# Side work of a hybrid decoder layer issued in the order of how it uses the matmul array: halves of columns, halves of rows, the whole array

## The chip, the core and the metric

The kernel runs on one core of one Trainium2 chip. The metric is the device time of one execution in microseconds (us). The engines that matter are PE (TensorE, the matmul array), DVE (VectorE), ACT (ScalarE), POOL (GpSimd) and SP (SyncE, which issues most of the DMAs). Each works through its own instructions in the program's order and meets the others only at semaphores.

## The reference

One pre-norm decoder layer on x of 512 positions by 1024 features, in float32:

```
u = rmsnorm(x);  proj = u @ w_in            # q, k, v, pool_in, z, xbc, dt, gates
y_a = dilated_attention(q, k, v) @ w_a      # 3 groups of 6 heads of 64, softmax with a bias
y_b = causal_pooling(pool_in) @ w_b
y_c = ssd(z, xbc, dt) @ w_c                 # Mamba-2 scan, 16 heads, 4 chunks of 128 positions
x = x + (g0 * y_a + g1 * y_b + g2 * y_c) @ w_o
x = x + conv_ffn(rmsnorm(x));  out = rmsnorm(x)
```

## The kernel before

The dense products are made of matmuls with 128x128 weights and 512 columns. Each float32 operand is split into a high and a low part, and a product is three runs of matmuls (high by high, high by low, low by high), all issued by `mm3` (L230). Their results are the tiles pa, pb, pqk, pu, ppw and p in four PSUM banks. A list of jobs, one for each block of weights, gives their order. Weights arrive by DMA (raw, L179), ACT rounds them (wh, L191), and DVE forms the low part (wl, L211), some jobs ahead. The program fixes by hand the order in which PE, ACT, DVE and POOL issue.

Attention, the SSD scan and the norms are side work, written as Python generators. After each chunk of the dense stream a job calls `step()`: it finishes the second halves of casts (`flush`), moves each running generator on to its next `yield`, oldest first, and then starts one new generator from `waiting`. So a generator's stages are spread over steps, and the steps' matmuls stand between the chunks of the stream.

Two kinds of generators meet the change most. An attention item (`item` in `attend`) is one head of a bank. The even head of a pair issues the scores of both heads (ps, L656), where each head uses 64 of the array's 128 rows. Each head then adds the bias and finds the maximum on DVE (L663, L664, L666, or L670, L674) and takes the exponential on ACT (L677). Two steps later the probabilities are transposed with the whole array (pt, L683), and DVE (even head) or ACT (odd head) copies them to SBUF (L684). One step after the odd head's transposes come the products with v (po, L695), where each head fills 64 of 128 columns, and ACT copies the result when it is complete (L701). An SSD item (`ssd_item`) fetches decay rows (al and ea, L913 and L919), transposes x (pxs, L923) and forms C by B (pcb, L929); DVE and ACT form a masked decay (L940, L941, L945); its last stage has products in halves of columns (py, L955), then whole products (pyo, L961; pst, L972), and DVE joins them (L963 to L977). Other whole-array side products are pcs, pact, pbt, pss, prb and the transposed statistics.

All side products share four further PSUM banks (tag "sm"): a product waits until the reader of an earlier tile has left its bank.

Of the kernel before, what the change touches and what calls it, by code (L numbers as in the profile page):

```python
# [83 lines left out]
def trunk(ctx: ExitStack, tc, out, x, rel_bias, ln1_g, w_in, b_gate, w_a, pool_w, pool_scale, w_b,  # L84
# [29 lines left out]
    def SM(name):  # L114
        return psum.tile([P, S], F32, name=name, tag="sm")
# [9 lines left out]
    waiting, running = [], []  # L125
# [13 lines left out]
    def flush():  # L139
        todo = second[:]  # L140
        second.clear()
        for f in todo:
            f()

    def step():
        flush()
        for it in list(running):
            try:
                next(it)
            except StopIteration:  # L150
                running.remove(it)
        if waiting:
            it = iter(waiting.pop(0))
            running.append(it)
            try:
                next(it)
            except StopIteration:
                running.remove(it)

    def after(n, it):  # L160
        for _ in range(n):
# [386 lines left out]
    def bias_of(g, h):  # L548
        if g == 0:
            return bias[h // 2][:, (h % 2) * 256:(h % 2) * 256 + 256]  # L550
        o = 256 * (g - 1) + (h % 2) * P
        return bias[3 + h // 2][:, o:o + P]
# [80 lines left out]
    def attend(g):  # L633
        nm = cpool.tile([P, 4, HEADS], F32, name=f"nm{g}")
        ls = cpool.tile([P, 4, HEADS], F32, name=f"ls{g}")
        if g == 0:
            banks = [[(1, 0, 2), (2, 1, 2)], [(3, 2, 2), (0, 0, 1)]]
        else:
            banks = [[(n, n, 1) for n in range(4)]]
        outs, probs, scores = {}, {}, {}  # L640

        def item(h, nb, bank):
            c, hh = h // 2, h % 2
            b = bias_of(g, h)
            off, spans = 0, []
            for n, kb, w in bank:
                spans.append((n, kb, w, off))
                off += w * P
            if hh == 0:

                q, k = QK["q", g, c], QK["k", g, c]
                pss = [SM("ps"), SM("ps")]
                for n, kb, w, o in spans:
                    for i in range(2):
                        r = slice(DH * i, DH * i + DH)
                        pe.matmul(pss[i][:, o:o + w * P], q[r, n * P:(n + 1) * P],  # L656
                                  k[r, kb * P:(kb + w) * P], start=True, stop=True)
                scores[c, nb] = pss
            ps = scores[c, nb][hh]
            total = off  # L660
            sb = T("sb")
            if g == 0 and total == 384:
                dve.tensor_tensor(sb[:, :256], ps[:, :256], b, OP.add)  # L663
                dve.tensor_tensor(sb[:, 256:384], ps[:, 256:384], b[:, P:], OP.add)  # L664
                for n, kb, w, off in spans:
                    dve.tensor_reduce(nm[:, n, h:h + 1], sb[:, off:off + w * P],  # L666
                                      AX.X, OP.max, negate=True)
            else:
                n = len(bank)
                dve.tensor_tensor(sb.rearrange("p (n c) -> p n c", n=n),  # L670
                                  ps.rearrange("p (n c) -> p n c", n=n),
                                  b.unsqueeze(1).to_broadcast([P, n, S // n]), OP.add)
                n0 = bank[0][0]
                dve.tensor_reduce(nm[:, n0:n0 + n, h], sb.rearrange("p (n c) -> p n c", n=n),  # L674
                                  AX.X, OP.max, negate=True)
            for n, kb, w, off in spans:
                act.activation(sb[:, off:off + w * P], sb[:, off:off + w * P], AF.Exp,  # L677
                               bias=nm[:, n, h:h + 1], accum_out=ls[:, n, h:h + 1])
            yield
            yield  # L680
            pt = SM("pt")
            for o in range(0, total, P):
                pe.transpose(pt[:, o:o + P], sb[:, o:o + P], eye)  # L683
            (act.copy if h % 2 else dve.tensor_copy)(sb[:, :total], pt[:, :total])  # L684
            probs[h, nb] = sb
            if h % 2 == 0:
                return
            yield
            if c not in outs:
                outs[c] = SM("po")  # L690
            po = outs[c]
            for n, kb, w, off in spans:
                for i in range(w):
                    for hh in range(2):
                        pe.matmul(po[DH * hh:DH * hh + DH, n * P:(n + 1) * P],  # L695
                                  V[g, kb + i][:, (2 * c + hh) * DH:(2 * c + hh + 1) * DH],
                                  probs[2 * c + hh, nb][:, off + i * P:off + (i + 1) * P],
                                  start=i == 0, stop=i == w - 1)
            if nb == len(banks) - 1:
                o = T(f"o{g}")  # L700
                act.copy(blocked(o, g), grouped(po, g))  # L701
                OT[g, c] = o

        def stats():
            for src, store, nme in ((nm, NM, "nmT"), (ls, LS, "lsT")):
                ps = SM("pst")
                for n in range(4):
                    pe.transpose(ps[:HEADS, n * P:(n + 1) * P], src[:, n, :], eye)
                t = T(nme)
                dve.tensor_copy(blocked(t[:HEADS], g), grouped(ps[:HEADS], g))  # L710
                store[g] = t
            return
            yield

        fill([item(2 * c + hh, nb, bank) for c in range(3) for nb, bank in enumerate(banks)
              for hh in range(2)] + [after(2, stats())])

    AO = []
# [109 lines left out]
    def ssd_prep():  # L828
# [33 lines left out]
        dve.scalar_tensor_tensor(v4(a), v4(dtv), -1.0, bc(1), OP.mult, OP.mult)  # L862
        yield
        yield
        ps = SM("pcs")
        pe.matmul(ps[:, :n16], tri, a, start=True, stop=True)
        pe.matmul(ps[:, n16:2 * n16], ones, a, start=True, stop=True)
# [7 lines left out]
        act.activation(dec, dec, AF.Exp)  # L875
        act.activation(tot, tot, AF.Exp)
        yield
        pt = SM("pact")
        for c in range(4):
            pe.transpose(pt[:SH, c * P:(c + 1) * P], acs[:, c * SH:(c + 1) * SH], eye)  # L880
        at, et = T("acst"), T("east")
# [13 lines left out]
    btok, prev, done = {}, {}, set()  # L895

    def btok_item(gi):
        ps = SM("pbt")
        for c in range(4):
            pe.transpose(ps[:, c * P:(c + 1) * P], XS[8 + gi][:, c * P:(c + 1) * P], eye)  # L900
        t = btok[gi] = T("btok")
        act.copy(t, ps)
        return
        yield

    def ssd_item(c, gi):
        cs = slice(c * P, (c + 1) * P)
# [7 lines left out]
        if c:  # L915
            ea = T("ea")
            for i in range(2):
                h0 = 8 * gi + i
                sp.dma_start(ea[DH * i:DH * i + DH].rearrange("p (j l) -> p j l", j=4),  # L919
                             ed[h0:h0 + 8 - i:2, cs].partition_broadcast(DH))  # L920
        ps = SM("pxs")
        for j in range(4):
            pe.transpose(ps[:, j * P:(j + 1) * P], XS[4 * gi + j][:, cs], eye)  # L923
# [28 lines left out]
        for j in range(4):  # L952
            for i in range(2):
                o, lo = (2 * j + i) * DH, (2 * j + i) % 4 * P
                pe.matmul(py[DH * i:DH * i + DH, j * P:(j + 1) * P], xc[:, o:o + DH],  # L955
                          als[j // 2][:, lo:lo + P], start=True, stop=True)
        by_j = lambda t: t.rearrange("p (j l) -> p j l", j=4)
        if c:
            po = SM("pyo")
            for j in range(4):  # L960
                pe.matmul(po[:, j * P:(j + 1) * P], prev[gi][:, j * P:(j + 1) * P], XS[10 + gi][:, cs],  # L961
                          start=True, stop=True)
            dve.tensor_tensor(ea, po, ea, OP.mult)  # L963
            dve.tensor_tensor(ea, ea, py, OP.add)
# [49 lines left out]
    def y_norm(gi):  # L1014
        while len(SQ[gi]) < 4:
            yield
        yield
        yield
        ps = SM("pss")
        for tb in range(4):  # L1020
            pe.matmul(ps[:, tb:tb + 1], SQ[gi][0][:, tb * P:(tb + 1) * P], ones[:, :1],
                      start=True, stop=True)
        r = rstd_of(ps[:, :4], 4, S)
        dg = T("dg")
        dve.tensor_tensor(dg.rearrange("p (b t) -> p b t", b=4), eye.unsqueeze(1).to_broadcast([P, 4, P]),
                          r.unsqueeze(2).to_broadcast([P, 4, P]), OP.mult)
        yield
        yield
        yield
        ps = SM("prb")  # L1030
        pe.matmul(ps, ones, dg, start=True, stop=True)
        for j in range(4):
            y, m = Y[gi][:, j, :], 4 * gi + j
            dve.scalar_tensor_tensor(y, y, cst["dgc"][:, 8 + m:9 + m], ps, OP.mult, OP.mult)
            yh, yl = T("yth", F32R), T("ytl", F32R)
            act.copy(yh, y)
            YT[m] = (yh, yl)
            if j % 2:
                yield
                for q in (m - 1, m):  # L1040
                    dve.tensor_sub(YT[q][1], Y[gi][:, q % 4, :], YT[q][0].bitcast(F32))
# [614 lines left out]
```

## Time and profile before

| | |
|---|---|
| median of 3 runs | 1048.81 us (1046.5 to 1051.13) |
| the profiled execution, its own time | 1049.47 us |
| its span, first to last instruction | 1047.4 us |
| mean granted clock of PE | 0.997 |
| instructions | 13090, of which 5220 matmuls |

In the timeline of an engine each row gives the start in us from the start of the span, the duration in us, the engine, the source line, the operation, the output and inputs by the program's names, and the number of equal instructions merged into the row; a bracket gives idle time before it and what ended that. The form 64*128 or 128*64 of a matmul is rows by columns of the array in use. A matmul's duration includes its passage through the array, so starts are compared, not durations.

### The profile page before, as it was taken

Reading aid. Unit: us, or ns where it says so; the run is one execution under the profiler, and the core shown is the slowest. Engines: PE = TensorE matmul, PEld = TensorE weight load, DVE = VectorE, ACT = ScalarE, POOL = GpSimd, SP = SyncE. Lnnn points to the kernel's source line nnn. Section 1 sums busy time; section 2 is a strip of 40 time slices with the busy share of each in tenths; the row PEclk is TensorE's granted clock in tenths of the full one; section 3 lists DMA queues with packets and bytes.
Section 4 is the critical chain, followed back from the end, with each engine's and each line's share of the span. In section 5 each row is a group of like instructions: output and inputs, shape, how many; then the busy total and the mean of one; then the engine's idle time right before and its main releaser. Section 6 shows DMA issues by size and latency. Waiting matters only on the chain.

```text
span 1047.4 us, 13090 instructions
## 1 busy us (share of the span) xinstructions
PE 1036.3 (99%) x5220; PEld 864.5 (83%) x5220; DVE 642.6 (61%) x865; ACT 467.6 (45%) x753; POOL 138.0 (13%) x118
## 2 busy tenths in 40 slices
PE   8999999999999999999999999999999999999997
PEld 8988877898888887787888888898888888878885
DVE  4563565774356647676658856766766566556645
ACT  5432555452474363557554324545444343433331
POOL 1680000000000001100143500001111111110110
PEclk9999999999999999999999999999999999999999
DMA  8445222127222363542252426643232322362322
GB/s 254 145 111 152 97 65 74 31 59 202 81 81 81 82 159 101 152 130 59 65 151 81 161 81 223 222 156 107 81 121 81 116 86 89 112 241 66 115 101 81
DMA packets 119787, 121.80 MB, mean 116 GB/s; under 512 B 5523, under 2 KB 101590, under 8 KB 119727
## 3 DMA queue, kind: packets, MB, share of 16 engines
q1 hardware_dynamic: 119135, 120.12, 37.1%
q8 instruction: 41, 0.67, 0.3%
q10 hardware_dynamic: 592, 0.86, 0.3%
q14 instruction: 19, 0.16, 0.0%
HBM read 115.07 MB, written 4.32 MB: 114 GB/s over the span
## 4 chain that ended last, share of the span: by engine, by line
PE 92%; DVE 3%; DMA 2%; ACT 2%; issue 0%; DVEq 0%; SPq 0%; ACTq 0%
PE pa L230 35%; PE pu L230 22%; PE pb L230 13%; PE pqk L230 9%; PE pa L1508 2%; PE p L230 2%; DVE wl L211 2%; PE ps L656 1%; PE po L695 1%; PE pt L683 1%; DMA raw<-in_ffn_w_up_dram 1%; PE ppw L230 1%; ACT wh L191 1%; PE py L955 1%; DMA raw<-in_w_o_dram 1%; PE pyo L961 1%
## 5 line engine op out<-in xcount | busy, mean ns | idle before, releaser
L211 DVE TENSOR_TENSOR wl<-raw,wh 128x2048 fp32r<-128x2048 f32 (+3 forms) x95 | 218.5, 2301 | 77.7 <-ACT wh L191 40.3
L191 ACT CAST wh<-raw 128x1024 fp32r<-128x1024 f32 (+3 forms) x188 | 189.6, 1026 | 67.4 <-DVE raw L333 21.1
L230 PE MATMUL pa<-uh,wh 128*128 128x512 f32 x384 | 98.7, 399 | 0.0
L1165 DVE SCALAR_TENSOR_TENSOR hc<-pu,fcol,hc 128x510 f32<-128x510 f32 x88 | 65.9, 748 | 50.8 <-ACT hc L1162 49.2
L230 PE MATMUL pa<-uh,wl 128*128 128x512 f32 x384 | 95.0, 389 | 0.0
L230 PE MATMUL pa<-ul,wh 128*128 128x512 f32 x384 | 94.9, 389 | 0.0
L230 PEld LDWEIGHTS pa<-ul,wh 128*128 128x128 f32 x384 | 72.1, 188 | 15.2
L230 PEld LDWEIGHTS pa<-uh,wl 128*128 128x128 f32 x384 | 72.0, 188 | 15.2 <-DVE wl L211 0.3
L230 PE MATMUL pu<-uh,wh 128*128 128x512 f32 (+1 forms) x352 | 83.7, 380 | 0.2 <-ACT uh L448 0.2
L230 PE MATMUL pu<-ul,wh 128*128 128x512 f32 (+1 forms) x352 | 83.5, 379 | 0.0
L230 PE MATMUL pu<-uh,wl 128*128 128x512 f32 (+1 forms) x352 | 83.5, 379 | 0.0
L230 PEld LDWEIGHTS pa<-uh,wh 128*128 128x128 f32 x384 | 70.2, 188 | 15.3 <-issue 1.0
L230 PEld LDWEIGHTS pu<-uh,wh 128*128 128x128 f32 x352 | 64.1, 188 | 12.8 <-ACT uh L448 0.4
L230 PEld LDWEIGHTS pu<-ul,wh 128*128 128x128 f32 x352 | 64.2, 188 | 12.5
L230 PEld LDWEIGHTS pu<-uh,wl 128*128 128x128 f32 x352 | 64.2, 188 | 12.5
L1162 ACT ACTIVATE hc<-pu,fcol,fcol 128x512 f32<-128x512 f32 x40 | 31.2, 780 | 75.5 <-PE pu L230 75.3
L1170 POOL TENSOR_TENSOR hc<-hc 128x512 f32<-128x512 f32 x22 | 31.5, 1432 | 223.6 <-DVE hc L1165 169.4
L934 POOL TENSOR_TENSOR xd<-xc,dec 128x512 f32<-128x512 f32 x6 | 6.4, 1065 | 360.1 <-DVE xc L925 334.5
L677 ACT ACTIVATE sb<-sb,nm 128x128 f32<-128x128 f32 (+1 forms) x72 | 30.1, 419 | 24.1 <-DVE nm L674 17.2
L1050 ACT ACTIVATE sg<-pa,col 128x512 f32<-128x512 f32 x24 | 16.5, 687 | 50.7 <-PE pa L230 50.6
L230 PE MATMUL pqk<-uh,wh 128*128 128x512 f32 x144 | 36.9, 394 | 0.0
L230 PE MATMUL pqk<-ul,wh 128*128 128x512 f32 x144 | 36.3, 389 | 0.0
(348 smaller groups left out, 1751.7 us busy)
## 6 DMA issues: line engine op xcount, KB each, us to landing
raw<-in_w_in_dram SPq DMA_DIRECT2D x25, 1024.0 KB
raw<-in_ffn_w_up_dram SPq DMA_DIRECT2D x22, 1024.0 KB
raw<-in_w_in_dram SPq DMA_DIRECT2D x20, 512.0 KB
raw<-in_ffn_w_down_dram SPq DMA_DIRECT2D x10, 1024.0 KB
raw<-in_w_o_dram SPq DMA_DIRECT2D x8, 1024.0 KB
raw<-in_w_b_dram SPq DMA_DIRECT2D x4, 1024.0 KB
al<-ad SPq DMA_DIRECT2D x16, 256.0 KB
raw<-in_w_c_dram SPq DMA_DIRECT2D x4, 1024.0 KB
```

What stands on the lines that cost most here:

```text
L191: act.copy(job.high[:, :, o], job.raw[:, :, o])
L211: (eng or dve).tensor_tensor(l[:, :, o], job.raw[:, :, o], h[:, :, o].bitcast(F32), OP.subtract)
L230: pe.matmul(ps, l, r, start=first and n == 0, stop=last and n == total - 1)
L656: pe.matmul(pss[i][:, o:o + w * P], q[r, n * P:(n + 1) * P], k[r, kb * P:(kb + w) * P], start=True, stop=True)
L677: act.activation(sb[:, off:off + w * P], sb[:, off:off + w * P], AF.Exp, bias=nm[:, n, h:h + 1], accum_out=ls[:, n, h:h + 1])
L683: pe.transpose(pt[:, o:o + P], sb[:, o:o + P], eye)
L695: pe.matmul(po[DH * hh:DH * hh + DH, n * P:(n + 1) * P], V[g, kb + i][:, (2 * c + hh) * DH:(2 * c + hh + 1) * DH], probs[2 * c + hh, nb][: ...
L1050: act.activation(s, ps, AF.Sigmoid, bias=col[:, o:o + 1])
L1162: act.activation(t, ps, AF.Identity, bias=ff["c1"][:, ff["b"] + m:ff["b"] + m + 1], scale=fw(2, m))
L1165: dve.scalar_tensor_tensor(t[:, sh:], ps[:, :S - sh], fw(k, m), t[:, sh:], OP.mult, OP.add)
L1170: pool.tensor_tensor(a, a, t, OP.mult)
L1508: pe.matmul(first[2 * n + j][:, lo:hi], a[:, k, j * P:(j + 1) * P], b[:, k, lo:hi], start=a is wh and b is uh and k == 0, stop=a is wl and ...
```

## The change

A generator may now yield a phase, `ROWS` or `WHOLE`, ahead of matmuls of that kind. `step()` takes the new generator in first, and then goes over all of them three times: in phase 0 each goes on until a bare `yield` (the end of its step) or until it names a later phase; those that named `ROWS` go on next, those that named `WHOLE` last. So all products in halves of columns of a step come first, then the scores, then everything that uses the whole array. Whatever a generator does for ACT, DVE, POOL or SP between these points moves with it. In particular, the odd head's bias, maximum and exponentials have no matmul before them, so they are issued in phase 0, ahead of the transposes and copies of older generators in the same step.

```diff
     def step():
         flush()
-        for it in list(running):
-            try:
-                next(it)
-            except StopIteration:
-                running.remove(it)
         if waiting:
-            it = iter(waiting.pop(0))
-            running.append(it)
-            try:
-                next(it)
-            except StopIteration:
-                running.remove(it)
+            running.append(iter(waiting.pop(0)))
+        now = [(it, 0) for it in running]
+        for phase in (0, ROWS, WHOLE):
+            now = [(it, advance(it, phase) if at == phase else at) for it, at in now]
+    ROWS, WHOLE = 1, 2
+    def advance(it, phase):
+        for at in it:
+            if at is None or at > phase:
+                return at
+        running.remove(it)
...
                 q, k = QK["q", g, c], QK["k", g, c]
+                yield ROWS
                 pss = [SM("ps"), SM("ps")]
...
             yield
             yield
+            yield WHOLE
             pt = SM("pt")
...
         def stats():
+            yield WHOLE
...
+        yield WHOLE
         ps = SM("pcs")
...
+        yield WHOLE
         pt = SM("pact")
...
     def btok_item(gi):
+        yield WHOLE
...
+        yield WHOLE
         ps = SM("pxs")
...
+        yield WHOLE
         if c:
             po = SM("pyo")
...
+        yield WHOLE
         ps = SM("pss")
...
+        yield WHOLE
         ps = SM("prb")
```

More of the change, by code (lines that the diff above doesn't have):

```diff
@@ L711, in stats @@
                 store[g] = t
-            return
-            yield
         fill([item(2 * c + hh, nb, bank) for c in range(3) for nb, bank in enumerate(banks)
@@ L902, in btok_item @@
         act.copy(t, ps)
-        return
-        yield
     def ssd_item(c, gi):
```

## The prediction

> **What bounds the kernel now.** I read the page first, for the engines' shares and the chain that ended last, and then PE's waits.
>
> ```profile
> PE 1036.3 (99%) x5220; PEld 864.5 (83%) x5220; DVE 642.6 (61%) x865; ACT 467.6 (45%) x753; POOL 138.0 (13%) x118
> ...
> PE 92%; DVE 3%; DMA 2%; ACT 2%; issue 0%; DVEq 0%; SPq 0%; ACTq 0%
> ```
> ```profile
> PE uT L1525 <- DVE v L1531: 2.2, 1, 2.2
> PE pa L1466 <- DVE relb L511: 1.1, 1, 1.1
> PE pb L230 <- DVE wl L211: 0.5, 1, 0.5
> PE pu L230 <- ACT uh L448: 0.2, 1, 0.2
> ```
>
> PE is never without work for long: its four waits add up to 4.0 us, none of them in the steps that this change touches. DVE at 61% and ACT at 45% have room. So whatever PE issues costs its time directly, and whatever makes PE wait in these steps is added to the span. The change removes no work. It can only shorten the passages between kinds of products, or bring waits that were not there.
>
> The next view is PE's timeline in the second attention group: one step with transposes alone, one with all three kinds, and the start of one with two.
>
> ```profile
> 295.16 1.98 PE L230 MATMUL pa<-uh,wl 128*128 128x512 f32 x8
> 296.98 0.60 PE L683 MATMUL pt<-eye,sb 128*128 128x128 f32 x4
> ...
> 301.09 1.97 PE L230 MATMUL pa<-uh,wl 128*128 128x512 f32 x8
> 302.99 1.09 PE L695 MATMUL po<-sb,vr 128*64 128x128 f32 x16
> 304.02 0.66 PE L683 MATMUL pt<-eye,sb 128*128 128x128 f32 x4
> 304.61 1.16 PE L656 MATMUL ps<-k,q 64*128 64x128 f32 x16
> 305.70 2.12 PE L230 MATMUL pa<-uh,wh 128*128 128x512 f32 x8
> ...
> 317.29 1.09 PE L695 MATMUL po<-sb,vr 128*64 128x128 f32 x16
> 318.32 0.66 PE L683 MATMUL pt<-eye,sb 128*128 128x128 f32 x4
> 318.73 1.64 PE L230 MATMUL pa<-uh,wh 128*128 128x512 f32 x6
> ```
> ```profile
> 152.51 0.88 PE L695 MATMUL po<-sb,v 128*64 128x128 f32 x12
> 153.31 0.66 PE L683 MATMUL pt<-eye,sb 128*128 128x128 f32 x4
> ```
>
> Eight dense matmuls that are followed by transposes take 1.82 us to the next start (295.16 to 296.98), and 1.90 us when products in halves of columns follow (301.09 to 302.99). Entering that kind costs 0.08 us. Sixteen such products take 1.03 us to the next start (302.99 to 304.02) and twelve take 0.80 (152.51 to 153.31), so four take 0.23, sixteen 0.92 at that rate, and some 0.11 to 0.13 is fixed, for the way in and out. One excursion into halves costs about 0.2 us in all. The Trainium skill, page "TensorEngine Tiling (Array Packing)", section Key Properties, says that changing the tiling mode drains the array; these rows agree, and 0.2 us is what they make of it.
>
> **What moves on PE.** I compared the order in which the two built programs issue. PE's instructions differ in ten steps and are the same everywhere else. Three steps (near 152, 172 and 303) go from po, pt, ps to po, ps, pt. One near 162 is the same with pact in front. Three (near 134, 290 and 457) swap pt and ps, with as many changes of kind as before. Two (near 464 and 495) go from py, pyo, po to py, po, pyo. One near 480 goes from py, pyo, pst, ps to py, ps, pyo, pst. The remaining differences follow from these.
>
> A three-kind step: before, po starts at 302.99 and the stream at 305.70, 2.71 us. After, po takes 1.03, ps 1.09 as now (304.61 to 305.70), and pt behind halves 0.41 as in 318.32 to 318.73; the sum is 2.53, so 0.18 saved, 0.54 in the three steps. No row shows ps right behind po. If the array passes from one kind of halves to the other without a drain, each saves some 0.1 more; if that passage costs as much as two, nothing is saved. I take the price of one, since each way in has about the same price in these rows. By that rule of the Trainium skill, a drain at any change of mode, the price would also be one.
>
> A step with py and po:
>
> ```profile
> 464.27 1.09 PE L955 MATMUL py<-al,xc 128*64 128x128 f32 x16
> 465.29 1.16 PE L961 MATMUL pyo<-xcv,st 128*128 128x128 f32 x8
> 466.38 1.09 PE L695 MATMUL po<-sb,vr 128*64 128x128 f32 x16
> 467.40 0.66 PE L923 MATMUL pxs<-eye,xs 128*128 128x128 f32 x4
> 467.95 0.49 PE L929 MATMUL pcb<-xcv 128*128 128x128 f32 x2
> 468.20 2.08 PE L230 MATMUL pa<-uh,wh 128*128 128x512 f32 x8
> ```
>
> Joining py and po saves one excursion, 0.2 us, in the step near 495. The step near 480 saves one change of four, half an excursion, 0.1. At 464 the saving meets a wait: in the new program pxs takes the bank that po leaves, so it waits for the copy of po on ACT, with only pyo between. Before, po came last and pxs used another bank. At best nothing waits and 0.2 is saved; at worst pxs waits about as long as pyo now takes (465.29 to 466.38, 1.09). I take a loss of 0.2, near the good end, because ACT's copy runs while pyo runs. The step near 162 has a like wait (pt takes a bank of the new scores, whose first reader is DVE), and I count its saving as used up. For it, the three swapped steps and small waits on banks that go I take 0.2 saved in all, between 0.6 saved and 0.2 lost.
>
> Saved so far: 0.54 + 0.2 + 0.1 + 0.2 = 1.04 us. Lost: 0.2.
>
> **What moves on ACT.** Here the change does more than it says. In a step in which an odd head's transposes are due and a new odd head enters, the older copy (L684) was issued first; now the new head's exponentials (L677) are. These wait for DVE's maximum (L674 or L666), and the copy, whose data has long been there, waits behind them in ACT's queue. The next step begins with po, whose second product reads that copy. So po, and behind it everything on PE, waits if the exponentials end late. The rows of the step before 317.29:
>
> ```profile
> 313.09 0.59 ACT L684 COPY sb<-pt 128x512 f32<-128x512 f32 x1
> 315.96 0.40 ACT L677 ACTIVATE sb<-sb,nm 128x128 f32<-128x128 f32 x1 [2.28 <-DVE nm L674]
> ...
> 317.13 0.39 ACT L677 ACTIVATE sb<-sb,nm 128x128 f32<-128x128 f32 x1
> ```
>
> The copy, at 313.09 now, comes after the last exponential: 317.13 + 0.39 = 317.52, done at 318.11. The product is due with po at 317.29. With some 0.1 for the first pair of po already issued, PE waits 0.71 us. The 2.28 us in which ACT stood idle before the exponentials, now free, will hold up the copy.
>
> The same before the po of 179.47:
>
> ```profile
> 176.86 0.59 ACT L684 COPY sb<-pt 128x512 f32<-128x512 f32 x1 [0.57 <-PE pt L683]
> ...
> 179.32 0.39 ACT L677 ACTIVATE sb<-sb,nm 128x128 f32<-128x128 f32 x1
> ```
> ```profile
> 179.47 1.09 PE L695 MATMUL po<-sb,v 128*64 128x128 f32 x16
> ```
>
> 179.32 + 0.39 + 0.59 = 180.30 against 179.47: with the same 0.1, a wait of 0.73.
>
> And before the po of 152.51, where DVE is busy with the SSD's small operations:
>
> ```profile
> 153.73 0.49 ACT L677 ACTIVATE sb<-sb,nm 128x256 f32<-128x256 f32 x1
> ```
> ```profile
> 142.83 0.56 DVE L684 COPY sb<-pt 128x384 f32<-128x384 f32 x1 [2.42 <-PE pt L683]
> 143.30 0.20 DVE L839 COPY dr<-dr 8x128 f32<-8x128 f32 x1
> ...
> 144.87 0.18 DVE L850 TENSOR_SCALAR dtu<-dtt 128x64 f32<-128x64 f32 x1
> ```
>
> Now these exponentials end only at 154.22. With the copy behind, po would wait until 154.81, 2.2 us. But DVE's order changes in favour: L839 to L666 (143.30 to 144.87, 1.57 us) move ahead of L684 into the 2.42 us in which DVE waited for pt, so what follows, the late maximum included, can come up to 1.57 earlier. The wait is between 0.6 and 2.2 us; part of the lead is lost because DVE then meets scores that PE has not yet formed, and I take 1.2.
>
> At the other copies moved in this way the exponentials end before po is due, as I read the same rows there, so they cost nothing; if DVE ran a microsecond later there, they would. The Trainium skill, "TensorEngine Tiling (Array Packing)", section PSUM Bottleneck, warns that tiling speeds up TensorE "but not PSUM evacuation"; L684 is such an evacuation, and the three waits above are how it speaks against this change.
>
> **What moves on DVE, POOL and SP.** DVE's L945 moves ahead of L963; it takes idle time in which DVE waited for pyo. POOL keeps its order. On SP one pair of al loads is issued before a fetch of weights rather than behind it, in time in which SP waits for DVE to release the raw buffer, and one al later stands behind a fetch instead of ahead. Both are wanted only steps later, so I price them at nothing; a fetch late by the length of such a load would still be hidden by the jobs that run ahead.
>
> **Sum.** 1.2 + 0.73 + 0.71 + 0.2 lost, 1.04 saved: 1.8 us slower. On the profiled execution's own 1049.47 us that makes 1051.3; that execution is 0.66 above the median of the runs, so against the median it is 1048.81 + 1.8 = 1050.6. A measurement of this kernel can tell about 0.5%, some 5 us, from no change; this sum is well inside it.
>
> **Rivals.** *The waits do not come* (ACT gets its maximum earlier, since DVE's queue is shorter at that point in each of the three steps). Then the savings are left: 1.0 us, or 1.6 if the passage from po to ps is free, so about 1047.6. For it: DVE has idle time in every such step. Against: the rows above, where the maximum comes late because its own inputs do. Chance 0.2.
>
> *Halves to halves saves nothing*, the passage costing as much as one over the whole array: 0.84 fewer saved in the steps with po or py beside ps, 1051.4. Nothing in the trace speaks to it. In such a case the reordering does not do what it is meant to, and the waits remain. Chance 0.1.
>
> *The queue on ACT slows the whole attention.* Eight copies of odd heads now stand behind exponentials. If each makes po wait as the first may at its worst (2.2) or as the others do (0.7), that is 3 x 2.2 + 5 x 0.7 = 10.1, less 1.0 saved, so 9 us: 1057.9. It becomes measurable from an average of about 0.8 us a copy (5.2 + 1.0 over eight). Against it: only three of the eight have exponentials that end near po or after it. For it: a late po also delays what DVE and ACT do next, and so the next copy. Chance 0.07.
>
> **Numbers.** The forecast, three waits and small savings, has the remaining 0.63; with the bounds (the first wait 0.6 to 2.2, the bank wait 0.2 saved to 1.1 lost, the passage free or double) it spans 1049 to 1053. The first rival reaches 1047, and the runs before alone spread by 2.3 us to either side of their median, so I take 1046.8 to 1053.6. A gain of over 0.5% has no case behind it but the spread of runs, 0.02; a loss of over 0.5% is the third rival, 0.07; the rest is no change that could be told, 0.91.
>
> **What would show it.** In the changed kernel's trace: PE waits on ACT's L684 ahead of po near 152, 179 and 318, of about 1.2, 0.7 and 0.7 us; a small wait of pxs on L701 near 467; the step near 304 shorter by 0.18, with ps 1.03 behind po; the step near 495 shorter by 0.2. If PE shows no new wait, the first rival is right; if po to ps takes 0.2 more than po to pt does now, the second; if po waits in most steps of attention, the third. A change of over 5 us either way, or a wait of the dense stream on wl or wh in these steps, would prove the whole working wrong.

## The result and the profile after

The changed kernel takes 1050.46 us (median of 22 runs) against 1048.96 for the kernel before (22 runs); the ratio is 1.0016, with a 95% interval of 1.0009 to 1.0023. It is slower by 1.7 us (0.9 to 2.4). Two of its 22 runs, of 1482.42 us (at a granted clock of 0.654) and of 3685.86 us, are left out of the ratio; the other 20 have a median of 1050.34. Its profiled execution takes 1050.77 us, with a span of 1048.7.

The part of the span ahead of the first side products differs between the traces, also between kernels that issue the same there: from the first product uT, near 8.5 us, to the first dense product behind the second group of them (L1508 in the kernel before) it is 3.94 to 5.57 us. So spans are not compared below, but the cost of each step: the start of the seventh matmul of the dense stream behind the side products, less the start of the last one ahead of them, less seven times 0.227 us, the distance at which dense matmuls start. A step of attention or of the SSD that nothing touches gives the same cost in all traces to within some 0.03 us. Times of a step are those of the kernel before (152, 179, 317), though later kernels reach it a microsecond or two earlier or later.

The page of the changed kernel, its engines, and then PE's waits:

```profile
PE 1035.2 (99%) x5220; PEld 864.4 (82%) x5220; DVE 642.9 (61%) x865; ACT 466.8 (45%) x753; POOL 138.5 (13%) x118
```
```profile
PE po L701 <- ACT sb L690: 2.2, 3, 1.1
...
PE pt L689 <- DVE sb L675: 0.2, 1, 0.2
```

The shares are those of before. One row is new and large: po waits three times for ACT's copy of an odd head (L690, which was L684). The row gives idle time behind the modelled end of the product before, and so less than the steps lose: the three steps together cost 3.44 us more than they would without the waits. Their rows, PE and ACT in turn:

```profile
152.08 0.43 PE L701 MATMUL po<-sb,v 128*64 128x128 f32 x2
153.60 0.87 PE L701 MATMUL po<-sb,v 128*64 128x128 f32 x10 [1.09 <-ACT sb L690]
154.40 0.92 PE L661 MATMUL ps<-k,q 64*128 64x256 f32 x8
155.26 0.66 PE L689 MATMUL pt<-eye,sb 128*128 128x128 f32 x4
```
```profile
152.10 0.51 ACT L682 ACTIVATE sb<-sb,nm 128x256 f32<-128x256 f32 x1 [3.40 <-DVE nm L679]
...
152.60 0.49 ACT L682 ACTIVATE sb<-sb,nm 128x256 f32<-128x256 f32 x1
...
153.09 0.45 ACT L690 COPY sb<-pt 128x384 f32<-128x384 f32 x1
```
```profile
180.07 0.43 PE L701 MATMUL po<-sb,v 128*64 128x128 f32 x2
181.16 1.09 PE L701 MATMUL po<-sb,v 128*64 128x128 f32 x14 [0.66 <-ACT sb L690]
```
```profile
180.54 0.56 ACT L690 COPY sb<-pt 128x512 f32<-128x512 f32 x1
```
```profile
318.76 0.43 PE L701 MATMUL po<-sb,vr 128*64 128x128 f32 x2
319.61 1.09 PE L701 MATMUL po<-sb,vr 128*64 128x128 f32 x14 [0.41 <-ACT sb L690]
```
```profile
318.99 0.56 ACT L690 COPY sb<-pt 128x512 f32<-128x512 f32 x1
```

Each time po has issued two products when it stops, and goes on as the copy ends (153.54, 181.10, 319.55). The copy starts where the last exponential of the new head ends, and ACT had stood idle ahead of those exponentials, waiting for DVE's maximum: for 3.40 us near 152, 3.13 near 179 and 2.77 near 317.

The other side, the step with three kinds near 303 and the one with py and po near 464:

```profile
304.63 1.09 PE L701 MATMUL po<-sb,vr 128*64 128x128 f32 x16
305.65 1.16 PE L661 MATMUL ps<-k,q 64*128 64x128 f32 x16
306.75 0.66 PE L689 MATMUL pt<-eye,sb 128*128 128x128 f32 x4
307.16 1.19 PE L234 MATMUL pa<-uh,wh 128*128 128x512 f32 x4
```
```profile
466.34 1.09 PE L962 MATMUL py<-al,xc 128*64 128x128 f32 x16
467.27 1.04 PE L701 MATMUL po<-sb,vr 128*64 128x128 f32 x16
468.24 1.16 PE L969 MATMUL pyo<-xcv,st 128*128 128x128 f32 x8
469.50 0.66 PE L930 MATMUL pxs<-eye,xs 128*128 128x128 f32 x4
470.18 0.49 PE L936 MATMUL pcb<-xcv 128*128 128x128 f32 x2
```

From po to the stream it is 307.16 - 304.63 = 2.53 us, against 2.71 before. ps follows po at 1.02, as pt did. Near 464 po follows py at 0.93, where pyo followed it at 1.02, and then pxs follows pyo at 1.26, where po followed it at 1.09.

### The profile page after: what moved, and what is told of

The parts are those of the page before. It is cut to its first block, busy times and chain, and to the rows that moved or that the text cites. A ratio compares the mean times of both kernels' runs of the same rounds, so it can differ in the third digit from the quotient of the medians.

```text
span 1048.7 us, 13090 instructions
## 1 busy us (share of the span) xinstructions
PE 1035.2 (99%) x5220; PEld 864.4 (82%) x5220; DVE 642.9 (61%) x865; ACT 466.8 (45%) x753; POOL 138.5 (13%) x118
## 4 chain that ended last, share of the span: by engine, by line
PE 93%; DVE 2%; ACT 2%; DMA 1%; issue 0%; ACTq 0%; DVEq 0%
PE pa L234 33%; PE pu L234 22%; PE pb L234 17%; PE pqk L234 9%; PE pa L1518 2%; PE p L234 2%; PE ps L661 1%; PE ppw L234 1%; PE po L701 1%; PE pt L689 1%; PE py L962 1%; DMA raw<-in_ffn_w_up_dram 1%; DMA eye<-in_c_eye_dram 1%; ACT wh L195 1%; PE uT L1535 1%; PE pyo L969 1%
```

## The experiments

### The copy first, with PE's order kept

```diff
                 scores[c, nb] = pss
+            else:
+                yield WHOLE
             ps = scores[c, nb][hh]
```

> The changed kernel, but a new odd head names WHOLE before its bias, maximum and exponentials, so that these are issued behind the older odd head's copy L684, as in the kernel before. PE's order is that of the changed kernel, instruction by instruction. Theory 1 (the three waits of po are the copy standing behind the exponentials in ACT's queue; the order on PE by itself only saves): the steps near 152, 180 and 318 get back 1.5, 1.1 and 0.85 us, the step near 152 then costs 2.3, the ones near 180 and 318 1.5 and 1.6; some 3.4 us less than the changed kernel, 1.0 to 1.5 less than the kernel before, about 1047.5 us against 1048.8. Rival A (po waits because the products before it moved, or because DVE's order changed): the waits stay, within 0.5 us of the changed kernel. Rival B (the first rival of the prediction, turned round: the waits go but the savings on PE were noise): level with the kernel before within 0.3 us in the sum over the steps.

Measured: 1047.83 us against 1048.93 before, ratio 0.9984 (0.9976 to 0.9993). PE's waits:

```profile
PE pxs L932 <- ACT o L709: 0.3, 1, 0.3
PE pt L691 <- DVE sb L677: 0.2, 1, 0.2
```

No wait of po is left. The steps near 152, 179 and 317 cost 2.28, 1.53 and 1.64 us, where the changed kernel has 3.79, 2.61 and 2.49; all others are the same in both to 0.02. That is 3.44 us between two kernels with the same order on PE, and 1.3 us below the kernel before in the sum over the steps. On DVE the two differ only near 141, 157, 440 and 472, in none of the three steps. Theory 1 holds, with its size: the order on PE saves 1.3 us, the order on ACT loses 3.4. Rivals A and B fall. This version beats both kernels.

### The queue alone, with PE's order of before

```diff
     def step():
         flush()
-        for it in list(running):
...
+        order = list(running)
         if waiting:
-            it = iter(waiting.pop(0))
+            new = waiting.pop(0)
+            it = iter(new)
             running.append(it)
+            order.insert(0 if new in odd else len(order), it)
+        for it in order:
...
```

> The kernel before with its order on PE instruction by instruction; only a new odd head's bias, maximum and exponentials are issued at the start of its step, ahead of the older generators, as the changed kernel does. Theory 1: po waits for ACT's copy near 152, 179 and 317 by about 1.5, 1.1 and 0.85 us, and nothing is saved: 3 to 3.5 us slower than the kernel before, about 1052.2 us. At 152 it may be less, since the odd head's maximum is here ahead of the SSD's small operations. Rival A (it needs the new order of products): no new wait, level with the kernel before within 0.5 us. Rival C (the queue costs more where po is late in its step): PE hides part of it behind other side products, under 2 us.

Measured: 1050.45 us against 1048.93, ratio 1.0014 (1.0004 to 1.0024). In the steps only the one near 317 is longer, by 0.85 us; near 152 and 179 nothing waits, and theory 1's 3 to 3.5 us did not come. So the copy stands behind the exponentials at all three places, and that is not enough. DVE and ACT ahead of the po of 179, in this kernel and then in the changed one:

```profile
176.90 0.60 DVE L665 TENSOR_REDUCE nm<-sb 128x1 f32<-128x256 f32 x2
177.42 1.28 DVE L399 TENSOR_TENSOR uf<-uh,ul 128x512 f32<-128x512 f32 x2
```
```profile
178.24 0.56 ACT L683 COPY sb<-pt 128x512 f32<-128x512 f32 x1
```
```profile
177.47 1.29 DVE L404 TENSOR_TENSOR uf<-uh,ul 128x512 f32<-128x512 f32 x2
178.67 0.42 DVE L668 TENSOR_TENSOR sb<-ps,b 128x256 f32<-128x256 f32 x1
...
179.20 0.60 DVE L671 TENSOR_REDUCE nm<-sb 128x1 f32<-128x256 f32 x2
```

Here the maximum is ahead of uf (1.28 us on DVE), so the copy ends at 178.80 and po, due at 179.20, finds it done. In the changed kernel the maximum is behind uf. The experiment had moved more than ACT's queue: it put the odd head ahead of every generator, on DVE too. The next two take that apart.

### PE's order of before, ACT and DVE as changed

```diff
...
+        new = waiting.pop(0) if waiting else ()
+        running.append(iter(new))
+        if new in odd:
+            now = [(it, advance(it, 0)) for it in list(running)]
+            for it, at in now:
+                if at:
+                    advance(it, WHOLE)
+        else:
+            for it in list(running):
+                advance(it, WHOLE)
...
```

> PE's order is that of the kernel before, instruction by instruction. In a step in which an odd head enters, the order on ACT and DVE is that of the changed kernel: first the generators that name no phase, then the odd head's bias, maximum and exponentials, then the stages that use the whole array, the older copy L684 among them. The earlier kernel with the queue alone put the odd head ahead of every generator, so its maximum also overtook L400 (1.28 us on DVE ahead of the po at 179) and the SSD's small operations (ahead of the po at 152); there po waited only near 317. Theory 1, refined (the wait is the copy behind exponentials whose maximum is late, and the maximum is late by what stands ahead of it on DVE): all three waits return, 1.5 us at 152, 1.1 at 179, 0.85 at 317, and with nothing saved that makes 3.4 us in the steps against the kernel before, about 1052.3. Rival A (the new order on PE is needed for the waits at 152 and 179): only the 0.85 at 317.

Measured: 1052.22 us against 1048.45, ratio 1.0036 (1.0024 to 1.0048), 3.8 us slower.

```profile
PE po L706 <- ACT sb L695: 1.9, 3, 1.1
```

All three waits are back: the steps cost 1.49, 0.84 and 0.84 us more than before, 3.17 in all. Theory 1 as refined holds, and the waits need nothing of the new order on PE, so rival A falls. The one near 179 is 0.84 and not 1.08, which the part on the prediction takes up. The step near 405 is also 0.49 longer, since the loads of al came late there (DVE's L954 waits for them until 408.71).

### The changed kernel with the maximum first

```diff
+        order = list(running)
         if waiting:
-            running.append(iter(waiting.pop(0)))
-        now = [(it, 0) for it in running]
...
+            order.insert(0 if new in odd else len(order), it)
+        now = [(it, 0) for it in order]
...
```

> The changed kernel with PE's order unchanged, instruction by instruction, and with the copy still behind the exponentials on ACT; only the odd head's bias, maximum and exponentials go ahead of the generators that name no phase, so that the maximum does not stand behind L400 on DVE near 179 nor behind the SSD's small operations near 152. Theory 1, refined: the waits of po near 152 and 179 go (1.5 and 1.1 us), the one near 317 stays (0.85), where only the convolution's own operations stand ahead; 2.6 us less than the changed kernel, about 1047.9. Rival A (the copy's place in ACT's queue alone decides): all three waits stay, level with the changed kernel.

Measured: 1047.26 us against 1048.45, ratio 0.9990 (0.9980 to 0.9999).

```profile
PE po L705 <- ACT sb L694: 0.4, 1, 0.4
```

One wait is left, near 317 (0.83 us more than without); near 152 and 179 the steps cost 2.28 and 1.53, as with the copy first. All steps together cost 2.6 us less than in the changed kernel, as theory 1 had it, and rival A falls. So the wait is a product of two orders: the copy behind the exponentials on ACT, and the maximum behind other work on DVE. Undoing either of the two removes the waits near 152 and 179. Near 317 DVE has only the convolution ahead of the maximum, which moving the odd head does not change; there the copy itself has to move, ahead of the exponentials or, as the next kernel shows, to DVE.

### Odd copies on DVE

```diff
-            (act.copy if h % 2 else dve.tensor_copy)(sb[:, :total], pt[:, :total])
+            dve.tensor_copy(sb[:, :total], pt[:, :total])
```

> The changed kernel with its order, but the copy L690 of odd heads is on DVE like that of even heads, right behind the new odd head's maximum and beside its exponentials instead of behind them. Theory 1, refined: the wait is then from DVE's queue alone. Near 317 the maximum ends at 317.31 and a copy of 0.68 ends at 317.99, before po at 318.76: no wait. Near 152 the maximum ends at 151.97, the copy of 384 columns (0.56) at 152.5, po is due at 152.08 and its second pair at 152.24: a wait of 0.3. Near 179 the maximum ends at 179.72, the copy at 180.40, the second pair is due at 180.23: 0.2. Some 2.9 us less than the changed kernel, about 1047.6. Rival J (odd copies on DVE push its wl and later maxima back, and other products wait): new waits of PE on DVE in other steps of attention, level with the changed kernel or above.

Measured: 1048.44 us against 1047.94, ratio 1.0004 (0.9995 to 1.0013). The steps near 152, 179 and 317 cost 2.78, 1.91 and 1.64: waits of 0.50, 0.38 and none. The places are as forecast, and the two sizes were taken 0.2 too small: they were counted from the second start of po, 0.16 us behind the first, and the part on the prediction shows that products issued ahead of a stop save nothing. The other steps cost what they cost in the changed kernel, to 0.1, so rival J falls; the remedy is weaker than the copy first.

### The price of a passage: po and ps in turn

```diff
...
-            for n, kb, w, off in spans:
+            for part, (n, kb, w, off) in enumerate(spans):
+                if part:
+                    yield 2 * part
...
```

The scores ps take the phases between, `2 * part + 1`.

> As the kernel with the copy first, but in a step that has both po and ps their products alternate: one span of po, one of ps, the next of po, and so on. The step near 303 then passes seven times between halves of columns and halves of rows instead of once, the three steps near 152, 162 and 171 three times instead of once. Theory 1 (the passage between the two kinds of halves costs what a change from or to the whole array costs, about 0.1 us): the step near 303 gets 0.6 us longer, the other three 0.2 each, 1.2 in all, against the kernel with the copy first. Rival D (the passage is free): no difference, and the three-kind steps would have been able to save 0.1 more. Rival E (the passage costs two, the prediction's second rival): 1.2 and 0.4, 2.4 in all.

Measured: 1049.57 us against 1048.93, ratio 1.0001 (0.9992 to 1.0010), against 0.9984 for the kernel that it is made from. The step near 303:

```profile
303.32 0.44 PE L707 MATMUL po<-sb,vr 128*64 128x128 f32 x4
303.69 0.49 PE L663 MATMUL ps<-k,q 64*128 64x128 f32 x4
304.11 0.44 PE L707 MATMUL po<-sb,vr 128*64 128x128 f32 x4
...
306.48 0.66 PE L693 MATMUL pt<-eye,sb 128*128 128x128 f32 x4
```

The same products now take 306.48 - 303.32 = 3.16 us to the start of pt, against 306.75 - 304.63 = 2.12 in the changed kernel: 1.04 more for six passages, 0.17 each. Four products take 0.37 us (po) and 0.42 (ps) to the next start of the other kind, and 0.22 within a run of one kind, so a passage into po costs 0.15 and one into ps 0.20. The steps near 152, 162 and 171 are 0.33, 0.35 and 0.33 longer, two passages each, again 0.17. Rival D, a free passage, falls. The total, 2.06, lies between theory 1 (1.2) and rival E (2.4), so it needs the price of a change from or to the whole array in the same measure.

### The price of a passage: po and pt in turn

The edit is as above, with the transposes of pt in place of ps.

> As the kernel with the copy first, but in a step that has both po and pt their products alternate: one span of po, one transpose of pt, and so on; ps then comes behind both. The step near 317 passes seven times between halves of columns and the whole array instead of once. Theory 1 (an excursion into halves costs 0.2 us, both ways together): the steps near 317 and 495 get 0.6 us longer each (three excursions more), the one near 179 0.2 longer; those with ps as well get their halves of rows behind whole products again, 0.1 to 0.2 more each. In all 2 to 3 us against the kernel with the copy first. Rival F (an excursion costs by the products' drain, so that four transposes spread out cost less than that, because each short transpose hides one way): under 0.3 us in the step near 317. Rival G (a change costs more when little work lies between two changes): over 1.2 us there.

Measured: 1051.67 us against 1048.93, ratio 1.0023 (1.0014 to 1.0031). The step near 317:

```profile
318.84 0.44 PE L707 MATMUL po<-sb,vr 128*64 128x128 f32 x4
319.21 0.33 PE L693 MATMUL pt<-eye,sb 128*128 128x128 f32 x1
...
321.18 2.10 PE L234 MATMUL pa<-uh,wh 128*128 128x512 f32 x8
```

From po to the stream it is 2.34 us; with po and pt in one piece each it was 318.73 - 317.29 = 1.44 before. Six passages cost 0.90 to 0.91, 0.15 each, 0.30 for an excursion. The steps near 141 and 179, with one excursion more, are 0.30 longer, the one near 495 (six passages) 0.85. All steps together cost 4.6 us more than with the copy first, where 2 to 3 were expected. So theory 1 has the mechanism right and the price too low by a third. Rival F falls with the 0.91 us. Rival G had over 1.2 us, and falls too: joining py and po near 495, with whole runs of products between the passages, saves 0.29, the same price for an excursion as with one transpose between. Against this price the passage between the two kinds of halves, 0.17, is that of one, not of two. The Trainium skill, "TensorEngine Tiling (Array Packing)", section Key Properties, says that changing the tiling mode drains the array. Both prices agree with that; the traces show the price of a passage, not the drain itself.

### The bank near 464

Three more kernels, made from the one with the copy first, go after the 0.3 us for which pxs waits there. First po ahead of py:

```diff
...
+        yield COLS2
         py = SM("py")
...
```

`COLS2` is a new phase behind 0 and ahead of `ROWS`.

> The kernel with the copy first, and in a step with po and py the po comes first (py names a phase of its own between them). The order on ACT and DVE stays. Theory 1 (pxs near 464 waits for ACT's copy of po, so with py between po and pyo there is 1 us more for it): the wait of pxs, 0.3 us, goes, and the step near 464 costs 0.45 less, 3.83, as the excursion saved is 0.29; the step near 495 is unchanged; 0.4 us less in all, about 1047.4. Rival H (another reader holds the bank, or pcb waits in place of pxs): the step stays at 4.28.

Measured: 1047.00 us against 1048.45, ratio 0.9983 (0.9974 to 0.9993); the step costs 4.29 us, as with the copy first (4.28). ACT in that step:

```profile
462.19 1.28 ACT L1063 ACT_TABLE_LOAD   x1
463.49 0.69 ACT L1063 ACTIVATE sg<-pa,col 128x512 f32<-128x512 f32 x1
464.07 1.04 ACT L195 CAST wh<-raw 128x1024 fp32r<-128x1024 f32 x1
465.01 1.09 ACT L709 COPY o<-po 128x512 f32<-128x512 f32 x1
```

po, at 462.78, is done a microsecond before the copy starts. The copy stands behind a cast, sg and a table load, and starts 2.23 us behind the first of the products in halves, as it did with py in front; where po lies makes no difference. The 0.45 us did not come, and rival H has the cost of the step. Then the copy on DVE:

```diff
-                act.copy(blocked(o, g), grouped(po, g))
+                (dve.tensor_copy if (g, c) == (2, 0) else act.copy)(blocked(o, g), grouped(po, g))
```

> The kernel with the copy first, and the copy of po to o (L709 in that kernel) of the one head pair that is due near 464 is issued on DVE instead of ACT. With po ahead of py the wait of pxs had stayed at 0.3 us, because on ACT the copy stands behind a table load (1.28 us), sg (0.69) and a cast (1.04) and starts at the same distance from the dense stream, whenever po ends; DVE stands idle there for 4.2 us. Theory 1 (the wait of pxs is ACT's queue once more): the wait goes and the step near 464 costs 4127 - 290 = 3.84 us instead of 4.28, with 0.45 less in all than the kernel with the copy first, about 1047.2 us. Rival H (another bank or reader holds pxs): 4.28 stays. Rival I (DVE's copy delays ea L973, and pcb or the next step's products wait for it): the wait turns up at another product of the same step.

Measured: 1050.45 us against 1047.94, ratio 1.0021 (1.0009 to 1.0032). The step costs 6.45, 2.16 more; rival I is right:

```profile
464.85 1.10 DVE L709 COPY o<-po 128x512 f32<-128x512 f32 x1 [4.37 <-PE po L703]
465.79 2.12 DVE L954 TENSOR_TENSOR al<-al,cbt 128x512 f32<-128x512 f32 x2
467.83 0.68 DVE L973 TENSOR_TENSOR ea<-pyo,ea 128x512 f32<-128x512 f32 x1
```

DVE's 4.37 us of idle time were not free. L954, whose data was ready, used to run ahead of them; now it stands behind a copy that waits for po, and ea, which frees the bank of pyo for pcb, stands behind L954. The same fault that the change made on ACT, made again on DVE. Last, the copy behind L954:

```diff
...
+                if (g, c) == (2, 0):
+                    yield ROWS
                 o = T(f"o{g}")
...
```

> The kernel with the copy first, with the o copy of the pair near 464 on DVE as in the kernel before this one, but issued behind the products al by cbt (L954, 2.12 us for two) instead of ahead of them; ahead of them it had waited for po and held them, and with them ea, up for 2 us. Theory 1 (an operation that waits holds up whatever stands behind it on its engine; here nothing but ea does): the copy starts 2.02 us behind the start of py, lasts 1.1 and ends as pyo's result comes, so ea starts 3.1 behind py as it did with the copy on ACT; pxs doesn't wait, and pcb, due 3.66 behind py in the bank that ea's 0.69 leave, waits up to 0.15. The step near 464 costs 3.84 to 4.0 us instead of 4.28; 0.3 to 0.45 less in all than the kernel with the copy first, about 1047.3 us. Rival I (DVE has no room for that copy at all): pcb or a later product waits, and the step costs 4.28 or more.

Measured: 1048.07 us against 1049.39, ratio 0.9992 (0.9983 to 1.0000). The step costs 4.28 again, not 3.84 to 4.0. The loss of 2.16 is gone, so the order on DVE was its cause. PE and DVE in turn:

```profile
466.31 0.66 PE L934 MATMUL pxs<-eye,xs 128*128 128x128 f32 x4
466.97 0.49 PE L940 MATMUL pcb<-xcv 128*128 128x128 f32 x2
```
```profile
465.15 1.10 DVE L711 COPY o<-po 128x512 f32<-128x512 f32 x1 [3.16 <-PE po L703]
466.23 0.69 DVE L975 TENSOR_TENSOR ea<-pyo,ea 128x512 f32<-128x512 f32 x1
```

pxs starts as DVE's copy ends (466.25), and pcb as ea ends (466.92): two small waits in place of one. The second sets the step. ea ends 3.79 us behind the first of the products in halves (463.13 here), and so it does with the copy first and with po first; pcb starts at 3.84 to 3.86 in all three. So the wait of pxs, which all three kernels went after, cost at most 0.02 of its own. Without either wait pcb would be due at 3.39 by estimate, the 3.68 of the kernel before (464.27 to 467.95) less the 0.29 saved. That pcb waits in place of pxs was the second half of rival H. What another order of the banks would give was not tried.

## Why the prediction was right, and where its steps were off

The time came out as forecast, 1050.46 us against 1050.6 and a loss of 1.7 us against 1.8, and for the forecast's reason: three waits of po outweigh what the array saves. The runs tell this loss from none, finer than the 0.5% that the prediction took for the limit. The terms, in us, from the costs of the steps:

| term | predicted | measured |
|---|---|---|
| wait near 152 | +1.2 | +1.51 |
| wait near 179 | +0.73 | +1.08 |
| wait near 317 | +0.71 | +0.85 |
| the three steps po, ps, pt | -0.54 | -0.60 |
| py and po joined, near 495 | -0.2 | -0.29 |
| near 480 | -0.1 | -0.19 |
| near 464 | +0.2 | +0.16 |
| near 162 and the swapped steps | -0.2 | -0.18 |
| near 405, al loads | 0 | -0.21 |
| sum | +1.8 | +2.13 |

The steps' 2.13 lies within the 0.9 to 2.4 of the runs. Part of the agreement is luck: the waits were taken 0.8 too small and the savings 0.5 too small, and the two errors cancel in part.

**An excursion was sized at 0.2 and costs 0.30.** The prediction took the slope between twelve products (0.80) and sixteen (1.03) for the price of four, and saw the way in only in the start of the first. In the traces pairs of po start 0.11 us apart; the first start of a new kind comes 0.09 to 0.10 late, and the interval that follows it is 0.05 to 0.10 longer once more. That second part was counted as work. It is why joining py and po gives 0.29, and the passage into ps, which the three-kind steps lose, 0.2.

**The waits near 179 and 317.** The copy's end, forecast 0.82 us behind the start of po near 317, came 0.79 behind it. Two things were left out. First, 0.1 was taken off for the products already issued, and they save nothing: the fourteen behind the stop take as long to the next start (181.16 to 182.18, 1.02 us) as sixteen without one. Products in halves start in pairs, 0.007 us apart; the stop splits a pair, and the last two start one by one. With the 0.06 from the copy's end to the next start of po that makes 0.85 near 317; near 179, with PE's order of before, 0.84 was measured. Second, near 179 the 0.21 saved in the step near 171 was lost again. The maximum there, in the kernel before (the row of the changed one is shown above):

```profile
178.37 0.60 DVE L666 TENSOR_REDUCE nm<-sb 128x1 f32<-128x256 f32 x2
```

From the po of the step near 171 (171.03 before, 171.85 after) to the end of the maximum it is 7.94 us before and 7.95 after: from the first result of that step on, DVE works up to the maximum without a pause of note. PE reaches the next po in 8.22 us instead of 8.44. PE came sooner to a wait that doesn't move: 0.84 + 0.21 is 1.05 of the 1.08.

**The wait near 152.** Of the lead of up to 1.57 us that DVE's new order gives, 0.70 remained. The maximum, before and after:

```profile
152.50 0.69 DVE L674 TENSOR_REDUCE nm<-sb 128x2 f32<-128x512 f32 x1
```
```profile
151.37 0.69 DVE L679 TENSOR_REDUCE nm<-sb 128x2 f32<-128x512 f32 x1
```

It ends 0.68 us behind the start of po before (152.51), and 0.02 ahead of it after (152.08). 2.2 less 0.70 is 1.5, inside the bounds of 0.6 and 2.2 but not at the 1.2 taken.

**The term at nothing near 405.** An al load that is issued ahead of a fetch of weights was priced at nothing. Before, DVE's L940 waited there for al (until 406.24, and again until 407.34), with ea behind it, which ends at 408.80, and pcb behind ea, at 408.86; now al is in time, pcb no longer waits, and the stream goes on 0.2 sooner. It is the same kind of queueing on SP, here to the good.

**The rivals.** The waits came, so the first is out; its 1047.6 is about what the kernel with the copy first takes (1047.83), which is that rival made true. The second is out by the two kernels with products in turn, the third because only three of the eight copies are late, those that the rows named. They are late by their place in ACT's queue and not by their length: the kernel with the copy first has the same copies, and po waits for none. The Trainium skill, "PSUM — Partial Sum Buffer", section "Engine vs sequencer instructions", calls the queues of ScalarE and VectorE strictly first in, first out. The three waits, and the 2.16 us on DVE near 464, are what that costs here.

## What to carry to other kernels

Sort side work by its use of the array only on the array's own queue: a phase that also moves the other engines' instructions changes who waits behind whom. For every engine, look at what a moved instruction waits for and put whatever is ready ahead of it; a copy that frees a bank or feeds the next products belongs ahead of a new item's chain, and long idle time on an engine's row is no proof of room, if ready work would stand behind the newcomer. With the copies back in front, the same sorting is worth 0.16% here; without, it costs 0.16%.

## What the runs showed of the hardware beyond what was expected

A passage between kinds of products costs 0.15 us between halves of columns (po) and the whole array (pt) and 0.17 between the two kinds of halves (po and ps), at 128 columns in float32, and a third to a half of it appears only behind the first products of the new kind. The price goes by the kind that is entered: into po 0.15, into ps 0.20 in the kernel with po and ps in turn. And time saved on PE ahead of a wait that another engine's chain sets is not saved: the 0.21 us near 171 came back in full at the next po.
